# Block differences of weights on GpSimd in place of VectorE, and four seven-product units in place of three in two projection pairs

## The chip, the cores and the metric

The kernel runs on one core of one Trainium2 chip. A core has five engines with a queue of instructions each, which run in order and wait for one another by semaphores: TensorE (PE in the profile; its weight loads are PEld), VectorE (DVE), ScalarE (ACT), GpSimd (POOL) and SyncE (SP, which here only starts transfers). Transfers between the chip's memory (HBM, where the kernel's DRAM tiles lie) and the core's working memory (SBUF) run on 16 DMA engines; they are started from SP's queue and from POOL's. Matrix products are accumulated in banks of a second memory (PSUM).

The metric is the device time of one execution in microseconds (us). The kernel before took 1457.91 us, the median of three runs (1455.56 to 1463.55).

## What is computed

One layer of a decoder trunk on 256 tokens of width 2048, all in float32: a mixer with two attention branches and gates, and a gated feed-forward part with a convolution of width 3.

```python
D_MODEL = 2048; SEQ = 256; D_FF = 5632

def hybrid_mixer(h, w_in, mla_q_norm, mla_w_q_up, mla_kv_norm, mla_w_kv_up,
                 swa_sinks, rel_table, w_o_mla, w_o_swa, w_out):
    c_q, c_kv, k_r, q_s, k_s, v_s, gates = jnp.split(h @ w_in, offsets, axis=-1)
    ...
    o_a = mla_attention(q[..., :MLA_NOPE_DIM], q_rope, kv[..., :MLA_NOPE_DIM], k_rope, kv[..., MLA_NOPE_DIM:])
    o_b = swa_attention(q_s, k_s, v_s, swa_sinks, rel_table)
    g = jax.nn.sigmoid(gates).reshape(B, S, N_BRANCHES, D_MODEL)
    merged = g[:, :, 0] * (o_a @ w_o_mla) + g[:, :, 1] * (o_b @ w_o_swa)
    return merged @ w_out

def conv_ffn(h, w_up, conv_w, conv_b, w_down):
    a, b = jnp.split(h @ w_up, 2, axis=-1)
    ap = jnp.pad(a, ((0, 0), (CONV_WIDTH - 1, 0), (0, 0)))
    c = conv_b
    for j in range(CONV_WIDTH):
        c = c + conv_w[j] * ap[:, j:j + S]
    return (jax.nn.gelu(c, approximate=True) * b) @ w_down

y = hybrid_mixer(rms_norm(x, norm_mix_pre), ...)
x = x + rms_norm(y, norm_mix_post)
y = conv_ffn(rms_norm(x, norm_ffn_pre), ...)
x = x + rms_norm(y, norm_ffn_post)
```

## The kernel before

**Tiling.** The 256 tokens are two tiles of 128. A projection runs over the rows of its weight matrix in blocks of 128 (`k`), and a matrix multiplication takes 128 rows by 128 tokens by 512 columns. Each float32 operand is split into a rounded high part and the remainder, so that one product is three matrix multiplications (`mm3`, lines 199 to 201): high times high, high times low, low times high.

**Chunks and their conversion.** Weights come in chunks of 128 x 1024 (512 KB). SP's queue starts the transfer into a raw tile (lines 143 and 172), ACT writes the high part (`whi`, line 164), and DVE subtracts it from the raw tile for the low part (`wlo`, line 165; both of its inputs lie in SBUF). Then PE multiplies. There are four pairs of `whi` and `wlo` in a ring (`RING = 4`) and three raw tiles (`RAW = 3`), with a few more tiles for one or the other in some stages. A chunk's conversion can start only when PE is done with the chunk four places ahead.

**Pairs and units.** In a "pair" (`pair_gemm`) 1024 columns are made at once. A unit is two row blocks (an even and an odd row chunk). A plain unit (`p` in an order such as `"ppspspsp"`) makes eight products: two row blocks, two token tiles, two column halves. A seven-product unit (`s`) makes seven: it takes sums of the token blocks (made by `token_sums` on DVE and ACT, ahead of time) and differences of the four weight blocks, and adds the partial results at the end (`end_sums`). The differences need four subtractions of 128 x 512. The order string says which units come first; the `s` units always take the first row blocks.

**Where the differences come from.** In two pairs they are made on the spot by `weight_sums` (lines 231 to 234): the gate pair (columns of `w_in`; tiles `gr` for the rows, `gta` and `gtb` for the differences, `cg` and `qg` for the PSUM banks) and the first pair of `w_out` (tiles `mr`, `yg`, `cw`, `qw`). There, POOL's queue starts the transfers of the rows (lines 326 and 327), and the differences are converted as a chunk would be. In the others they are parked: `park_sums` loads two row chunks into a staging tile (line 246, POOL's queue), four subtractions are made in place (line 253), and two stores (lines 258 and 263, POOL's queue) put the differences into DRAM tiles, from where `seven_parked` reads them as chunks later, in all 3.5 chunks for one `s` unit against 2 for a `p` unit. One park is called a quad of subtractions below. Parked are: the latent output pair `a_pair` (matrix `w_o_mla`, tiles `tw`, PSUM banks `ca` and `qa`), and the pairs of `ffn_w_down` (tiles `ta`, `tb` and `tc`, banks `cd`, `cdb`, `cdc`). All parks but the first four use one staging tile (tag `sg`), so that the next park's load waits until the one before has been stored.

**What sets the order.** The code is written against a counter of steps (`now`, `at`, `tick`); a step is one chunk of a projection. `park_sums` puts its subtractions at given steps (`t0` and `t0 + 1`), and the line `tc.keep_in_program_order` pins them to their place in the queue of the engine that makes them. Other instructions are put in order by the scheduler of the framework. At run time each queue goes on as soon as its semaphores let it.

**Stages**, by time in the profiled execution: sliding-window projections and attention to about 198 us; the first output block of that branch, 198 to 240; the gate pair, 240 to 282; the rest of that branch, to 350; latent attention with the other gates, to 550; the latent output pair, 551 to 593; the rest of that matrix with the merge, to 639; the first `w_out` pair, to 682; the rest and the norms, to 770; the first half of the feed-forward projection (steps c = 1 to 5), to 998; two pairs of `ffn_w_down`, to 1120; the second half, to 1340; the last two pairs, to the end.

Of the kernel before, what the change touches and what calls it, by code (L numbers as in the profile page):

```python
# [16 lines left out]
ALU = mybir.AluOpType  # L17
AX = mybir.AxisListType

P = 128  # L20
D = 2048
S = 256
NT = 2
# [19 lines left out]
def trunk_layer(ctx, tc, x, x_cols_in, conv_cols_in, g_mix_post, g_ffn_post, w_in, w_q, w_kv,  # L43
                sinks, rel, wo_a, wo_b, w_out, w_up, w_down, rope_tab, strip_sel, out):
    nc = tc.nc
    vec, act, pe, pool = nc.vector, nc.scalar, nc.tensor, nc.gpsimd
# [10 lines left out]
    base = ctx.enter_context(tc.tile_pool(name="base", bufs=1))  # L57
# [18 lines left out]
    def warm_up(n):  # L76
        for i in range(n):
# [6 lines left out]
                       base=0, channel_multiplier=1)  # L84
# [143 lines left out]

    def weight_sums(even, odd, ta, tb):
        a, b = slice(0, 512), slice(512, 1024)  # L230
        vec.tensor_tensor(ta[:, a], even[:, b], even[:, a], op=ALU.subtract)
        vec.tensor_tensor(ta[:, b], odd[:, b], even[:, b], op=ALU.subtract)
        vec.tensor_tensor(tb[:, a], odd[:, b], ta[:, a], op=ALU.subtract)
        vec.tensor_tensor(tb[:, b], odd[:, a], tb[:, a], op=ALU.subtract)

    staged = set()

    def park_sums(name, w, k, c0, pl, tag, t0, bufs=None):

        td = [dram.tile([P, 1024], F32, name=f"{name}{i}") for i in range(2)]  # L240
        st = []

        def load():
            st.append(sb(pl, [P, D], f"{name}s", tag=tag, bufs=bufs))
            for i in range(2):
                ins = pool.dma_start(st[0][:, i * 1024:(i + 1) * 1024], w[(k + i) * P:(k + i + 1) * P, c0:c0 + 1024])
                if tag not in staged:
                    tc.keep_in_program_order(ins)
            staged.add(tag)

        def less(o, x, y):
            o, x, y = (st[0][:, i * 512:(i + 1) * 512] for i in (o, x, y))
            tc.keep_in_program_order(vec.tensor_tensor(o, x, y, op=ALU.subtract))

        def even():
            less(0, 1, 0)
            less(1, 3, 1)
            pool.dma_start(td[0], st[0][:, 0:1024])

        def odd():  # L260
            less(3, 3, 0)
            less(2, 2, 3)
            pool.dma_start(td[1], st[0][:, 1024:2048])

        at(t0 - 5, load)
        at(t0, even)
        at(t0 + 1, odd)
        return td
# [444 lines left out]
    for g in range(4):  # L713
        acc = gemm(XH, XL, w_in, 0, KT, C_QS + 512 * g, 512)[0] if g else acc_q0
        swa_q(g, acc)
        b = now[0]
# [120 lines left out]
    tb = {0: gate_b(0)}  # L837
# [157 lines left out]
    b = now[0] + 2  # L995
# [8 lines left out]
    for j in range(4):  # L1004
        acc, _ = gemm(XH, XL, w_in, 0, KT, C_GA + 512 * j, 512)
        if j == 3:
            both = sb(base, [P, D], "ta3", tag="sg")
# [100 lines left out]
    yg_all = [[sb(p6, [P, 1024], f"yg_{t}_{j}", tag="f" + "ab"[t], bufs=2) for j in range(2)] for t in range(NT)]  # L1108
    yg = [[yg_all[t][j // 2][:, (j % 2) * 512:(j % 2 + 1) * 512] for j in range(4)] for t in range(NT)]
    ms = {}  # L1110
# [65 lines left out]
    w_done = [0]  # L1176

    def w_place():
# [5 lines left out]
        at(now[0] + 2, *(lambda k=k: late_loads(k) for k in range(4)))  # L1184
        return both[:, 0:1024], both[:, 1024:2048]

    def w_pair():
        d = [yg[t][j] for t in range(NT) for j in range(2)]
        c = pair_gemm("w", w_out, 0, 0, W_ORDER, lambda k, t: (MH_(k)[:, t * P:(t + 1) * P], ML_(k)[:, t * P:(t + 1) * P]),
                      lambda u: ms[u], 0, d, w_place, lambda: [yg_all[t][1] for t in range(NT)])  # L1190

        def pair_evac(i):
            t, j = divmod(i, 2)
            vec.tensor_tensor(d[i], d[i], c[i], op=ALU.add)
            act.activation(jk(f"yj{j}_{t}"), d[i], AF.Square, accum_out=ssy[t][:, j:j + 1])
            vec.tensor_tensor(d[i], d[i], gpost[0][:, j * 512:(j + 1) * 512], op=ALU.mult)

        for i in range(4):
            at(now[0] + i, lambda i=i: pair_evac(i))
# [334 lines left out]
    for i in range(4):  # L1534
        t, j = divmod(i, 2)
# [28 lines left out]


RING = 4
A_ORDER = "ppspspsp"
NA_ = A_ORDER.count("s")
GATE_ORDER = "psppspsp"
B_ORDER = "psspsspssp"  # L1570
B2_ORDER = "ppsspssppp"
NB2 = B2_ORDER.count("s")
# [79 lines left out]
```

## Time and profile before

| | |
|---|---|
| median of three runs | 1457.91 us |
| the profiled execution's own time | 1455.35 us |
| its span, first to last instruction | 1453.6 us |
| PE busy | 1443.9 us, 7522 matrix multiplications |
| DVE busy | 1162.5 us |
| ACT busy | 866.5 us |
| POOL busy | 113.6 us |
| subtractions for block differences, parked | 100 on DVE |
| the same, on the spot | 24 on DVE |

The page of the profile gives each engine's busy time, the share of each 40th of the span, the chain of work that ended last (followed back from the last instruction to what released it), and the costliest groups of instructions as `line engine operation out<-in`, with the count, the busy time, the mean duration in ns, and the idle time ahead of them with what ended it. A view by windows gives the busy time of each engine in a stretch of the span. The timeline gives instructions by start and duration, in brackets the idle time ahead and its releaser.

### The profile page before, as it was taken

The numbers are of one execution on the slowest core, as the hardware profiler recorded it, in microseconds if no ns is written. First come the engines' busy times: TensorE is split into PE (matmuls) and PEld (weight loads), VectorE is DVE, ScalarE is ACT, GpSimd is POOL, SyncE is SP. The second block draws the span as 40 slices with busy tenths as digits, with TensorE's granted clock in tenths as the row PEclk, the third lists the DMA queues.
The fourth block names the chain that finished last, engine by engine and source line by source line (L and its number), as shares of the span: only waits on it lengthen the run. The fifth ranks groups of instructions, "written<-read, shape, count | busy, mean of one in ns | idle before, by whom it ended". The sixth has DMA issues, their size and how long they took to land.

```text
span 1453.6 us, 21420 instructions
## 1 busy us (share of the span) xinstructions
PE 1443.9 (99%) x7522; PEld 1233.6 (85%) x7522; DVE 1162.5 (80%) x2034; ACT 866.5 (60%) x1422; POOL 113.6 (8%) x204
## 2 busy tenths in 40 slices
PE   9999999999999999999999999999999999999997
PEld 7888888888898888888888888888888888888886
DVE  7788896766878775888799899876777797986798
ACT  7588864544555655546576565655646565565673
POOL 0012110010000001100000011000000101010000
PEclk9999999999999999999999999999999999999999
DMA  8755376698775759975666898866878888788965
GB/s 301 218 171 163 104 262 193 218 325 292 245 218 175 231 155 321 353 232 177 216 207 212 266 335 302 279 208 213 310 271 268 307 276 291 248 282 275 356 216 208
DMA packets 164744, 359.74 MB, mean 247 GB/s; under 512 B 20843, under 2 KB 32012, under 8 KB 164636
## 3 DMA queue, kind: packets, MB, share of 16 engines
q1 hardware_dynamic: 143296, 282.76, 59.8%
q0 software_dynamic: 21248, 75.56, 15.1%
q8 instruction: 59, 0.97, 0.3%
q14 instruction: 49, 0.40, 0.1%
q10 hardware_dynamic: 92, 0.05, 0.0%
HBM read 323.67 MB, written 34.65 MB: 247 GB/s over the span
## 4 chain that ended last, share of the span: by engine, by line
PE 97%; DVE 1%; ACT 1%; issue 0%; DVEq 0%; ACTq 0%
PE ub L1345 10%; PE ua L1345 10%; PE accg L199 10%; PE accg L201 10%; PE accg L200 10%; PE ub L1349 5%; PE ua L1349 5%; PE cd L200 2%; PE cd L201 2%; PE cd L199 2%; PE cdc L200 1%; PE cdc L199 1%; PE cdc L201 1%; PE mpo L981 1%; PE cdb L200 1%; PE cdb L199 1%
## 5 line engine op out<-in xcount | busy, mean ns | idle before, releaser
L164 ACT CAST whi<-raw 128x1024 fp32r<-128x1024 f32 (+2 forms) x498 | 504.5, 1022 | 374.7 <-PE accg L201 107.6
L165 DVE TENSOR_TENSOR wlo<-raw,whi 128x1024 fp32r<-128x1024 f32 (+2 forms) x498 | 586.1, 1189 | 176.0 <-ACT whi L164 171.4
L199 PE MATMUL accg<-whi,ahl 128*128 128x512 f32 (+1 forms) x416 | 162.8, 391 | 0.0
L201 PE MATMUL accg<-whi,ahl 128*128 128x512 f32 (+1 forms) x416 | 160.7, 386 | 0.0
L200 PE MATMUL accg<-wlo,ahl 128*128 128x512 f32 (+1 forms) x416 | 159.9, 384 | 0.0
L1345 PE MATMUL ub<-ahl,whi 128*128 128x512 f32 x640 | 154.7, 391 | 0.0
L1345 PE MATMUL ua<-ahl,whi 128*128 128x512 f32 x640 | 154.6, 391 | 0.0
L1345 PEld LDWEIGHTS ub<-ahl,whi 128*128 128x128 f32 x640 | 117.5, 188 | 22.8 <-ACT cc L1237 0.2
L1345 PEld LDWEIGHTS ua<-ahl,whi 128*128 128x128 f32 x640 | 117.5, 188 | 22.7
L199 PE MATMUL accg<-whi,bhl 128*128 128x512 f32 x256 | 100.7, 393 | 0.0
L201 PE MATMUL accg<-whi,bhl 128*128 128x512 f32 x256 | 99.9, 390 | 0.0
L200 PE MATMUL accg<-wlo,bhl 128*128 128x512 f32 x256 | 99.8, 390 | 0.0
L201 PEld LDWEIGHTS accg<-whi,ahl 128*128 128x128 f32 x416 | 78.1, 188 | 15.5
L200 PEld LDWEIGHTS accg<-wlo,ahl 128*128 128x128 f32 x416 | 78.2, 188 | 13.2
L199 PEld LDWEIGHTS accg<-whi,ahl 128*128 128x128 f32 x416 | 78.2, 188 | 12.9
L1349 PEld LDWEIGHTS ub<-ahl,wlo 128*128 128x128 f32 x640 | 82.3, 191 | 3.2
L1349 PEld LDWEIGHTS ua<-ahl,wlo 128*128 128x128 f32 x640 | 82.2, 191 | 3.1
L1349 PE MATMUL ua<-ahl,wlo 128*128 128x256 f32 x640 | 83.7, 283 | 0.0
L1349 PE MATMUL ub<-ahl,wlo 128*128 128x256 f32 x640 | 83.3, 283 | 0.0
L201 PEld LDWEIGHTS accg<-whi,bhl 128*128 128x128 f32 x256 | 48.0, 188 | 10.1
L200 PEld LDWEIGHTS accg<-wlo,bhl 128*128 128x128 f32 x256 | 48.1, 188 | 9.7
L199 PEld LDWEIGHTS accg<-whi,bhl 128*128 128x128 f32 x256 | 48.1, 188 | 9.6
(660 smaller groups left out, 2682.7 us busy)
## 6 DMA issues: line engine op xcount, KB each, us to landing
raw<-in_ffn_w_up_dram SPq DMA_DIRECT2D x142, 512.0 KB, 4.8
raw<-in_w_in_dram SPq DMA_DIRECT2D x105, 512.0 KB, 4.6
raw<-in_ffn_w_down_dram SPq DMA_DIRECT2D x66, 512.0 KB, 5.7
xraw<-in_ffn_w_up_dram SPq DMA_DIRECT2D x34, 512.0 KB, 5.1
raw<-in_w_o_swa_dram SPq DMA_DIRECT2D x32, 512.0 KB, 4.8
raw<-in_w_o_mla_dram SPq DMA_DIRECT2D x26, 512.0 KB, 5.9
raw<-in_w_out_dram SPq DMA_DIRECT2D x26, 512.0 KB, 4.6
ta_s<-in_ffn_w_down_dram POOLq DMA_DIRECT2D x24, 512.0 KB, 6.2
```

Source lines behind the costliest of these rows:

```text
L164: act.copy(hi[:, a:b], raw[:, a:b])
L165: vec.tensor_tensor(lo[:, a:b], raw[:, a:b], hi[:, a:b].bitcast(F32), op=ALU.subtract)
L199: pe.matmul(o, ah, bh, start=start, stop=False)
L200: pe.matmul(o, ah, bl, start=False, stop=False)
L201: pe.matmul(o, al, bh, start=False, stop=stop)
L981: pe.matmul(o, w(t), p_[:, c], start=n == 0, stop=n == 5)
L1345: pe.matmul(acc[i], hi[:, c], hn[p][:, j * 512:(j + 1) * 512], start=p + j == 0, stop=stop)
L1349: pe.matmul(acc[i][:, 0:256], lo[:, c], hn[p][:, j * 512:j * 512 + 256], start=False, stop=False)
```

## The change

All subtractions of `weight_sums` and of `park_sums` are issued to GpSimd. The latent output pair's order goes from three `s` units and five `p` units to four and four, the gate pair's too; each gets one more set of token sums, and the latent output pair one more park. Since `w_out`'s pair would write all its differences to the same two tiles, its second `s` unit gets another tile (`wt`, in the staging tile's place).

```diff
     def weight_sums(even, odd, ta, tb):
         a, b = slice(0, 512), slice(512, 1024)
-        vec.tensor_tensor(ta[:, a], even[:, b], even[:, a], op=ALU.subtract)
-        vec.tensor_tensor(ta[:, b], odd[:, b], even[:, b], op=ALU.subtract)
-        vec.tensor_tensor(tb[:, a], odd[:, b], ta[:, a], op=ALU.subtract)
-        vec.tensor_tensor(tb[:, b], odd[:, a], tb[:, a], op=ALU.subtract)
+        pool.tensor_tensor(ta[:, a], even[:, b], even[:, a], op=ALU.subtract)
+        pool.tensor_tensor(ta[:, b], odd[:, b], even[:, b], op=ALU.subtract)
+        pool.tensor_tensor(tb[:, a], odd[:, b], ta[:, a], op=ALU.subtract)
+        pool.tensor_tensor(tb[:, b], odd[:, a], tb[:, a], op=ALU.subtract)
...
         def less(o, x, y):
             o, x, y = (st[0][:, i * 512:(i + 1) * 512] for i in (o, x, y))
-            tc.keep_in_program_order(vec.tensor_tensor(o, x, y, op=ALU.subtract))
+            tc.keep_in_program_order(pool.tensor_tensor(o, x, y, op=ALU.subtract))
...
+    def w_sums():
+        if w_done[0] % 2:
+            return [yg_all[t][1] for t in range(NT)]
+        both = sb(base, [P, D], "wt", tag="sg")
+        return both[:, 0:1024], both[:, 1024:2048]
+
     def w_pair():
         d = [yg[t][j] for t in range(NT) for j in range(2)]
         c = pair_gemm("w", w_out, 0, 0, W_ORDER, lambda k, t: (MH_(k)[:, t * P:(t + 1) * P], ML_(k)[:, t * P:(t + 1) * P]),
-                      lambda u: ms[u], 0, d, w_place, lambda: [yg_all[t][1] for t in range(NT)])
+                      lambda u: ms[u], 0, d, w_place, w_sums)
...
-A_ORDER = "ppspspsp"
+A_ORDER = "pspspssp"
 NA_ = A_ORDER.count("s")
-GATE_ORDER = "psppspsp"
+GATE_ORDER = "spspspsp"
```

Three places show how instructions move. The first is POOL's queue from the end of the `w_out` pair on (`gpost` are gains that are loaded there, `x_d` is the parked residual stream, `ta_0` and `ta_1` the two DRAM tiles of a park). Before:

```order
L1031 DMA gpost<-in_norm_mix_post_dram 128x512 x4
L1313 DMA x_d<-x_0_5938 128x512 x4
L1313 DMA x_d<-x_1_5939 128x512 x4
L258 DMA ta_0_7945<-ta_s 128x1024
L263 DMA ta_1_7946<-ta_s 128x1024
L246 DMA ta_s<-in_ffn_w_down_dram 128x1024 x2
```

With the change:

```order
L1031 DMA gpost<-in_norm_mix_post_dram 128x512 x4
L246 DMA ta_s<-in_ffn_w_down_dram 128x1024 x2
L253 TENSOR_TENSOR ta_s<-ta_s 128x512 x2
L258 DMA ta_0_7994<-ta_s 128x1024
L253 TENSOR_TENSOR ta_s<-ta_s 128x512 x2
L263 DMA ta_1_7995<-ta_s 128x1024
L246 DMA ta_s<-in_ffn_w_down_dram 128x1024 x2
```

The subtractions stand in POOL's own queue, between a park's load and its stores; nothing of another engine's step stands between one park and the next, and two parks now come ahead of the stores of the residual stream.

The second is DVE's queue in the gate pair (`wlo` from `gr` are the rows' own conversions, from `gta` and `gtb` those of the differences). Before:

```order
L165 TENSOR_TENSOR wlo_2959<-gr_2935,whi_2958 128x512
L165 TENSOR_TENSOR wlo_2966<-gta_2938,whi_2965 128x1024
L231 TENSOR_TENSOR gta_3142<-gr_3139 128x512
L165 TENSOR_TENSOR wlo_2976<-gtb_2939,whi_2975 128x1024
L232 TENSOR_TENSOR gta_3142<-gr_3139 128x512
L165 TENSOR_TENSOR wlo_2988<-raw_2985,whi_2987 128x1024
L165 TENSOR_TENSOR wlo_3006<-raw_3003,whi_3005 128x1024
L165 TENSOR_TENSOR wlo_3024<-raw_3021,whi_3023 128x1024
L165 TENSOR_TENSOR wlo_3042<-raw_3039,whi_3041 128x1024
L233 TENSOR_TENSOR gtb_3143<-gr_3139,gta_3142 128x512
L234 TENSOR_TENSOR gtb_3143<-gr_3139,gtb_3143 128x512
```

With the change:

```order
L165 TENSOR_TENSOR wlo_2923<-gr_2899,whi_2922 128x512
L165 TENSOR_TENSOR wlo_2930<-gta_2902,whi_2929 128x1024
L807 SCALAR_TENSOR_TENSOR tb_0_2707<-tb_0_2707,accg_0_2711 128x512
L807 SCALAR_TENSOR_TENSOR tb_1_2709<-tb_1_2709,accg_1_2712 128x512
L165 TENSOR_TENSOR wlo_2940<-gtb_2903,whi_2939 128x1024
L165 TENSOR_TENSOR wlo_2962<-raw_2959,whi_2961 128x1024
L165 TENSOR_TENSOR wlo_2980<-raw_2977,whi_2979 128x1024
L165 TENSOR_TENSOR wlo_3001<-gr_2995,whi_3000 128x1024
L165 TENSOR_TENSOR wlo_3015<-gr_2995,whi_3014 128x512
L165 TENSOR_TENSOR wlo_3022<-gta_2998,whi_3021 128x1024
L165 TENSOR_TENSOR wlo_3032<-gtb_2999,whi_3031 128x1024
```

The four subtractions between the conversions are gone from DVE, and the second `s` unit follows the first after two plain chunks instead of four.

The third is SP's queue in the latent output pair, at its last `s` units (`araw` is a raw tile of this stage). Before:

```order
L172 DMA raw_6192<-in_w_o_mla_dram 128x1024
L172 DMA raw_6210<-in_w_o_mla_dram 128x1024
L172 DMA raw_6228<-in_w_o_mla_dram 128x1024
L172 DMA araw<-in_w_o_mla_dram 128x512
L172 DMA raw_6248<-tw_0_3736 128x1024
L172 DMA raw_6260<-tw_1_3737 128x1024
L172 DMA araw<-in_w_o_mla_dram 128x1024
```

With the change:

```order
L172 DMA raw_6231<-in_w_o_mla_dram 128x1024
L172 DMA raw_6243<-in_w_o_mla_dram 128x512
L172 DMA raw_6252<-tw_0_3756 128x1024
L172 DMA araw<-tw_1_3757 128x1024
L172 DMA raw_6275<-in_w_o_mla_dram 128x1024
L172 DMA raw_6287<-in_w_o_mla_dram 128x512
L1034 DMA x_0_5969<-in_x_dram 128x512
L172 DMA araw<-tw_0_3758 128x1024
L172 DMA raw_6307<-tw_1_3759 128x1024
```

Two `s` units now stand next to each other: eight loads, seven chunks' worth, for two units, with no plain unit between them (the load of `x` among them is of the residual stream).

## The prediction

> **What bounds the kernel now.** I read the page's first part and its chain of waits first, then the chain's pieces in a steady stretch, then the groups of the two engines that feed PE.
>
> ```profile
> span 1453.6 us, 21420 instructions
> PE 1443.9 (99%) x7522; PEld 1233.6 (85%) x7522; DVE 1162.5 (80%) x2034; ACT 866.5 (60%) x1422; POOL 113.6 (8%) x204
> PE 97%; DVE 1%; ACT 1%; issue 0%; DVEq 0%; ACTq 0%
> L164 ACT CAST whi<-raw 128x1024 fp32r<-128x1024 f32 (+2 forms) x498 | 504.5, 1022 | 374.7 <-PE accg L201 107.6
> L165 DVE TENSOR_TENSOR wlo<-raw,whi 128x1024 fp32r<-128x1024 f32 (+2 forms) x498 | 586.1, 1189 | 176.0 <-ACT whi L164 171.4
> ```
>
> ```profile
> 879.56 3.65 PE ua L1345 x16
> ```
>
> PE is idle for 9.7 us of 1453.6, and 97% of the chain is PE. ACT's conversions wait for PE (374.7 us) and DVE's for ACT: the converters are ahead and held back by the ring. 16 full-width multiplications take 3.65 us, 0.228 each, which is PE's pace. So time leaves this kernel only with multiplications, and enters it wherever the converters fall so far back that PE runs dry. Taking work from DVE alone is worth nothing as long as this holds.
>
> How far ahead they are is the question. In a seven-product unit of the gate pair, where the ring's four places cover less PE time than in plain units:
>
> ```profile
> 263.10 1.23 DVE L165 TENSOR_TENSOR wlo<-gtb,whi 128x1024 fp32r<-128x1024 f32 x1 [1.49 <-ACT whi L164]
> 265.54 0.39 PE L200 MATMUL qg<-wlo,xs 128*128 128x512 f32 x1
> ```
>
> The conversion ends at 264.33 and PE reads it at 265.54: 1.2 us to spare, though DVE had idled 1.49 us just before. This is the margin in the tight places.
>
> **The change part by part.** *Removed from PE.* Two plain units become seven-product units: two products of three multiplications less, 6 x 0.228 = 1.4 us. It is on the path, so the time falls by 1.4.
>
> *Removed from DVE.* 124 subtractions, in 31 quads:
>
> ```profile
> L253 DVE TENSOR_TENSOR ta_s<-ta_s x48: 682/686/697, 290.3 to 937.9; 128x512 f32<-128x512 f32 x48
> L253 DVE TENSOR_TENSOR tb_s<-tb_s x24: 684/686/691, 1128.6 to 1243.6; 128x512 f32<-128x512 f32 x24
> L253 DVE TENSOR_TENSOR tc_s<-tc_s x16: 660/686/689, 494.2 to 1309.7; 128x512 f32<-128x512 f32 x16
> L253 DVE TENSOR_TENSOR tw_s<-tw_s x12: 681/685/692, 375.7 to 465.3; 128x512 f32<-128x512 f32 x12
> L231 DVE TENSOR_TENSOR gta<-gr x3: 679/684/693, 205.4 to 247.3; 128x512 f32<-128x512 f32 x3
> ```
>
> At 0.686 us a quad is 2.74 us and all are 85 us of DVE. Worth 0, since DVE waits for ACT and ACT for PE.
>
> *Added to POOL.* 33 quads (26 parks and 7 on the spot), 132 subtractions. The trace has no such operation of this size on POOL; it has one of half the width, and a copy:
>
> ```profile
> L705 POOL TENSOR_TENSOR bhl<-o,bhl x16: 722/740/1518, 78.2 to 197.4; 128x256 fp32r<-128x256 f32 x16
> L557 POOL COPY gmat<-gx 128x38 f32<-128x38 f32 x1 | 0.2, 215 | 0.8 <-DMA gx<-in_x_cols_dram 0.8
> ```
>
> From 0.215 us at 38 columns to 0.740 at 256 is 2.4 ns a column, so 512 columns take 0.74 + 256 x 0.0024 = 1.36 us. The bounds are 0.74 (width costs nothing) and 1.48 (all is width). I take 1.36: a quad is 5.4 us, all are 180 us, and POOL, busy 113.6 us, has room. [...]
>
> Why L705 reaches 1518 decides what this does to DVE:
>
> ```profile
> 95.77 1.52 POOL L705 TENSOR_TENSOR bhl<-o,bhl 128x256 fp32r<-128x256 f32 x1 [1.69 <-ACT bhl L704]
> 95.46 1.22 DVE L165 TENSOR_TENSOR wlo<-raw,whi 128x1024 fp32r<-128x1024 f32 x1
> 102.48 0.74 POOL L705 TENSOR_TENSOR bhl<-o,bhl 128x256 fp32r<-128x256 f32 x1 [5.19 <-ACT bhl L704]
> 102.83 1.47 DVE L165 TENSOR_TENSOR wlo<-raw,whi 128x1024 fp32r<-128x1024 f32 x1
> ```
>
> At 95.77 POOL starts 0.31 us into a conversion and takes 0.78 more than its 0.74, while the conversion keeps its 1.22. At 102.83 a conversion starts while POOL has 0.39 left and takes 0.25 more. So the two hold each other up, and the later one pays. [...] If DVE always comes second, a quad costs it the full 5.4 us (the upper bound); if POOL does, 0. Conversions alone run 586 us of 1453.6, and with the sums and the feed-forward's own operations DVE does two-input work somewhat over half the time, so I take 60%, 3.2 us a quad. Against the 2.74 it saves, DVE comes out even over the whole kernel. What remains is where the quads go.
>
> *Moved.* On DVE a quad stood at its planned step; on POOL a park follows the one before as soon as the staging tile is free. That cycle is two load issues (1.06), landing, four subtractions with some waiting (about 7), and a store's issue and landing:
>
> ```profile
> ta_s<-in_ffn_w_down_dram POOLq DMA_DIRECT2D x24, 512.0 KB, 6.2
> ta<-ta_s POOLq DMA_DIRECT2D x24, 512.0 KB, 5.2
> 737.04 2.53 POOL L1313 DMA_DIRECT2D x_d<-x  x4 [13.47 <-DVE x L1152]
> 790.97 0.54 POOL L258 DMA_DIRECT2D ta<-ta_s  x1 [51.41 <-DVE ta_s L253]
> 945.90 1.06 POOL L246 DMA_DIRECT2D tb_s<-in_ffn_w_down_dram  x2 [6.48 <-DMA ta<-ta_s]
> ```
>
> In sum 1.1 + 6.2 + 7 + 0.5 + 5.2 = 20 us. Before, the first park of this part was stored at 790.97, and the load of 945.90 waited for its subtractions until 1128.6. With the change two of the 17 parks pass before the residual stream's stores, which still wait for DVE until 737; the 15 left follow at 20 us each and end near 737 + 300 = 1037, inside the first down pair, which had none. The stages:
>
> ```profile
> 198.00:224.00 26.00, 26.00 (x119) 21.47 (x118) 26.00 (x59) 14.82 (x23) 2.40 (x5) 1.00 0.79 272
> 240.00:262.00 22.00, 22.00 (x98) 18.10 (x97) 14.71 (x17) 9.55 (x10) 3.22 (x6) 1.00 0.62 216
> 262.00:290.00 28.00, 28.00 (x124) 23.01 (x124) 21.49 (x23) 18.00 (x20) 1.06 (x2) 1.00 0.58 196
> 550.00:594.00 44.00, 44.00 (x196) 36.44 (x195) 28.38 (x30) 24.39 (x27) 4.45 (x9) 1.00 0.94 338
> 594.00:632.00 38.00, 38.00 (x181) 31.39 (x180) 34.67 (x52) 17.99 (x23) 5.87 (x11) 1.00 0.94 326
> 632.00:683.00 51.00, 51.00 (x231) 42.19 (x230) 41.38 (x49) 26.45 (x29) 2.67 (x5) 1.00 0.56 190
> 790.00:940.00 150.00, 150.00 (x863) 132.40 (x862) 133.28 (x233) 89.35 (x146) 16.01 (x30) 1.00 0.86 291
> 940.00:1000.00 60.00, 60.00 (x344) 52.88 (x343) 43.57 (x76) 33.68 (x57) 1.06 (x2) 1.00 0.71 235
> 1000.00:1040.00 40.00, 40.00 (x178) 32.95 (x177) 27.95 (x32) 22.65 (x29) 0.00 (x0) 1.00 0.69 233
> ```
>
> (After the stretch and its length: busy time and instructions of PE, PEld, DVE, ACT and POOL, granted clock, DMA share, GB/s.)
>
> - *Ahead of the gate pair* (198 to 224) DVE has no idle time. Two quads leave it and two come on POOL: +1 us by the 3.2, and the fourth token sums +2.5 more. It stays hidden by the plain chunks to 240; without that cover, 2 us.
> - *Gate pair* (240 to 290): the third and fourth quads and one park, where one quad stood. Each can use up the 1.2 us margin: 3 x (3.2 - 1.2 - what DVE's idle time, a quarter of the stretch, gives back). I take 1 us (0 to 4). The rows are loaded two units ahead, into two `gr` tiles, so the quads' own length is hidden; with one tile it would not be, 5.4 us a unit.
> - *Latent output pair* (551 to 593): a seven-product unit reads 1.5 chunks more, 0.79 MB, or 2.3 us at 338 GB/s, where DMA is at 0.94 and ACT already waits for it:
>
> ```profile
> ACT whi L164 <- DMA raw<-in_w_o_mla_dram: 10.2, 6, 3.7
> 601.90 1.06 POOL L246 DMA_DIRECT2D ta_s<-in_ffn_w_down_dram  x2 [4.73 <-DVE la L1069]
> ```
>
>   The 1 MB loaded at 601.90 now goes past 660, which helps only behind it. I take 1 us (0 to 3).
> - *Merge and `w_out`* (594 to 690): three quads leave, three come, the first moved up to 602, where DVE is 91% busy, and a park comes to about 671, at the pair's tight end. I take 1 us (0 to 4).
> - *Feed-forward, first half* (740 to 1000): 8 quads become about 13, so per 20 us DVE gives 3.2 in place of 2.9 to 940 (8 x 2.74 in 150 us), and 3.2 in place of 0 after, where DVE idles 16.4 of 60. 0 (0 to 2): the ring is the plain, deep one.
> - *First down pair* (998 to 1040): two parks, 6.4 us of DVE into 12 idle, 4.2 MB more of transfers, on 233 GB/s. I take 1 us (0 to 4). The second half of the feed-forward loses all its quads, for nothing.
>
> The sum is -1.4 + 1 + 1 + 1 + 0 + 1 = +2.6 us: 1455.35 + 2.6 = 1458.0 for an execution like the profiled one. That execution was 2.6 below the median shown, so the median goes from 1457.91 to 1460.5.
>
> **The rivals.** *All is absorbed.* DVE's waits stay inside the margin and only PE's work changes: 1457.91 - 1.4 = 1456.5. For it: not one wait of PE for DVE makes the chain's first 97%. Against: 1.2 us is less than one held conversion.
>
> *The lock makes DVE the bound* (slower). DVE comes second each time, since POOL's four subtractions follow each other: 5.4 us a quad. In the tight places, the three quads of the gate pair, two of merge and `w_out`, two of the first down pair, each then costs PE 5.4 less the margin of 1.2 and about 2 us of idle time: 7 x 2.2 = 15, less 1.4: 1471.5. It decides once a quad's hold on DVE passes what idle time and margin give, about 3.2. For it: DVE is 100% busy from 198 to 224 and 91% from 594 to 632. Against: the conversion at 95.46 shows POOL paying. [...]
>
> *Transfers run ahead into a full stage.* The latent output pair takes its 2.3 us in full and the parks at the first down pair delay its chunks by as much as they move beyond the 338 seen: 233 + 105 is at the limit, some 5 us. 1457.91 - 1.4 + 2.3 + 5 + 2 for the quads = 1465.8.
>
> *DVE's relief shows in PE.* Its 9.7 us of idle time, mostly at both ends, would have to go: 1450 at the very best.
>
> **How the numbers follow.** My sum 0.45, all absorbed 0.17, the lock 0.25, transfers 0.10, relief 0.03. About 0.5%, 7.3 us, is what I count as telling from no change. The first two lie within it (0.62); the lock and the transfers are above it (0.35). The likeliest case's own range is 1456.5 to 1465. The range given, 1455 to 1474, reaches to the lock's price and a little beyond it; what is left out are a larger hold at the top and the relief below.
>
> **What would show it.** Right: 7516 multiplications; lines 231 to 234 and 253 on POOL at 1.3 to 2 us each; line 165's mean above 1189; the last store of a park near 1037 in place of 1310; new idle time of PE, one or two us in all, in the gate pair, around 602, at 671 and past 1000. Wrong: no idle time of PE there (all absorbed); PE waiting for `wlo` many us, with line 165 above 1.4 us in those windows (the lock); PE behind ACT behind DMA at 575 to 600 or 1000 to 1040 (transfers); subtractions at 2 us and more even where DVE idles, which would make my price wrong.

## The result, and the profile after

The changed kernel takes 1495.15 us, the median of six runs (1490.31 to 1496.45), where the kernel before took 1457.62 on the same occasions (six runs, 1455.56 to 1463.55). The ratio is 1.0251, with a 95% interval of 1.0229 to 1.0273: it is slower by some 37 us, well above the range that was given. The profiled execution spans 1491.4 us.

The page of the changed kernel: its span, the engines' busy time, the engines' shares of the chain of waits, and two of the costliest groups (busy time and mean of one, then the idle time before them).

```profile
span 1491.4 us, 21411 instructions
PE 1457.1 (98%) x7516; PEld 1239.2 (83%) x7516; DVE 1192.5 (80%) x1926; ACT 866.7 (58%) x1428; POOL 339.4 (23%) x342
PE 80%; DVE 10%; DMA 4%; issue 3%; ACT 3%; DVEq 0%; ACTq 0%; SPq 0%
L165 DVE TENSOR_TENSOR wlo<-raw,whi 128x1024 fp32r<-128x1024 f32 (+2 forms) x498 | 626.3, 1271 | 192.2 <-ACT whi L164 186.3
L253 POOL TENSOR_TENSOR ta_s<-ta_s 128x512 f32<-128x512 f32 x48 | 81.8, 1705 | 45.5 <-DMA ta_s<-in_ffn_w_down_dram 43.8
```

PE does six multiplications less, and yet is busy 13 us longer. Its idle time rises from 9.7 us to 34.3 (1491.4 less 1457.1). DVE has 108 instructions fewer than before and is busy 30 us longer. A conversion (L165) takes 1.271 us on the mean in place of 1.189, and DVE, which held 1% of the chain, now holds 10%.

Where is it lost? Stretches of the stages that matter, before (first fence) and after (second); behind each loss the changed kernel does the same work later than the kernel before. Columns as in the prediction: stretch and length, busy time of PE, PEld, DVE, ACT and POOL, granted clock, DMA share, GB/s.

```profile
690.00:725.00 35.00, 34.95 (x158) 28.56 (x157) 24.81 (x37) 20.01 (x30) 2.18 (x4) 1.00 0.66 207
755.00:775.00 20.00, 20.00 (x90) 16.57 (x89) 20.00 (x27) 13.06 (x17) 0.00 (x0) 1.00 0.68 210
770.00:790.00 20.00, 20.00 (x119) 17.64 (x118) 16.78 (x27) 12.96 (x20) 0.00 (x0) 1.00 0.60 182
810.00:830.00 20.00, 20.00 (x120) 17.81 (x119) 18.39 (x35) 12.05 (x20) 2.14 (x4) 1.00 0.90 292
870.00:890.00 20.00, 20.00 (x118) 17.71 (x117) 19.61 (x38) 12.16 (x19) 2.13 (x4) 1.00 0.84 282
```

```profile
198.00:224.00 26.00, 22.69 (x95) 17.91 (x95) 25.86 (x45) 10.02 (x17) 13.98 (x13) 0.93 0.64 211
690.00:725.00 35.00, 33.72 (x148) 27.22 (x147) 29.53 (x28) 17.45 (x23) 16.80 (x13) 1.00 0.81 277
770.00:790.00 20.00, 20.00 (x90) 16.58 (x89) 18.47 (x19) 9.61 (x13) 9.25 (x8) 1.00 0.74 254
790.00:810.00 20.00, 19.55 (x107) 16.57 (x106) 19.84 (x21) 10.80 (x14) 12.05 (x8) 1.00 0.74 256
810.00:830.00 20.00, 13.78 (x70) 11.80 (x69) 17.96 (x29) 10.49 (x19) 7.86 (x8) 0.83 0.80 270
905.00:925.00 20.00, 20.00 (x115) 17.60 (x114) 19.66 (x31) 9.74 (x15) 8.69 (x10) 1.00 0.91 308
```

The two largest losses come where DVE's own work had left it no idle time before. In 198 to 224 us it was busy 26.00 of 26 (quoted in the prediction). What it does in about 777 to 808 of the changed kernel, the last steps of a normalisation (`hx`, L1268 and L1270) between conversions, it did in 755 to 775 before, busy 20.00 of 20 (above). PE runs dry behind that: in 810 to 830 it issues 70 multiplications where it issued 120. A full DVE alone isn't enough, though: the work of 870 to 890, where DVE was busy 19.61 of 20, is done in about 905 to 925 with GpSimd working beside it (8.69 us), and PE loses nothing.

What happens inside, on DVE's queue and on POOL's (start, duration, instruction):

```profile
799.91 2.08 DVE L165 TENSOR_TENSOR wlo<-raw,whi 128x1024 fp32r<-128x1024 f32 x1 [0.16 <-ACT whi L164]
801.91 1.79 DVE L418 TENSOR_TENSOR ahl<-hx,ahl 128x512 fp32r<-128x512 f32 x1
803.63 2.26 DVE L1270 TENSOR_TENSOR hx<-hx,row 128x512 f32<-128x512 f32 x1
805.81 2.32 DVE L165 TENSOR_TENSOR wlo<-raw,whi 128x1024 fp32r<-128x1024 f32 x1
808.05 0.68 DVE L418 TENSOR_TENSOR ahl<-hx,ahl 128x512 fp32r<-128x512 f32 x1
```

```profile
796.16 6.99 POOL L253 TENSOR_TENSOR ta_s<-ta_s 128x512 f32<-128x512 f32 x2 [4.45 <-DMA ta_s<-in_ffn_w_down_dram]
804.04 3.01 POOL L253 TENSOR_TENSOR ta_s<-ta_s 128x512 f32<-128x512 f32 x2
```

One quad holds four DVE instructions. Unheld they take 1.22 + 0.68 + 0.68 + 1.22 = 3.80 us; here they take 8.45, so 4.65 us are lost to the hold, in a place where DVE has nothing to spare. As soon as the quad is over, L418 takes its 0.68 again.

DVE is late after that, and two things follow. First the chain of waits behind it (start, duration, what), then PE:

```profile
808.73 2.27 DVE wlo L165 x2
811.00 0.03 DVE cc L1244
811.03 7.71 DMA raw<-in_ffn_w_up_dram
818.74 0.02 issue
818.77 0.02 ACTq L164
818.78 0.04 issue
818.82 1.05 ACT whi L164
```

```profile
809.62 1.11 PE L1355 MATMUL ua<-ahl,wlo 128*128 128x256 f32 x8
816.01 1.09 PE L1289 MATMUL fT<-ident,f 128*128 128x128 f32 x4 [5.28 <-DVE uu L1250]
816.75 2.06 PE L1355 MATMUL ua<-ahl,wlo 128*128 128x256 f32 x8
```

The late conversion gives its raw tile back late, so the next chunk's load lands late (7.71 us on the chain). And PE stands for 5.28 us before a transpose that waits for `uu`, the activation that DVE computes (L1244 to L1250). PE's multiplications keep the program's order here, so a converted chunk behind the transpose cannot help: eight of a chunk's sixteen L1355 run at 809.62, and the other eight start only at 816.75. The stall of 198 to 224 has the same form; its wait is

```profile
PE ckT L747 <- DVE ck L741: 2.6, 1, 2.6
```

(in total, times, longest): a transpose of the compressed key that DVE normalises. Here it isn't the conversions that are held, but six instructions of 128 x 2 elements with which DVE works out that key's norm. Four of them:

```profile
203.19 1.25 DVE L402 TENSOR_TENSOR ck_t<-ck_t,ck_ss 128x2 f32<-128x2 f32 x1
205.95 1.25 DVE L407 TENSOR_TENSOR ck_y<-ck_y,ck_t 128x2 f32<-128x2 f32 x1
207.33 2.94 DVE L401 TENSOR_TENSOR ck_t<-ck_y 128x2 f32<-128x2 f32 x1
212.31 1.25 DVE L410 TENSOR_TENSOR ck_u<-ck_u,ck_t 128x2 f32<-128x2 f32 x1
```

In the kernel before, with no subtraction on GpSimd, each takes 0.15 or 0.16 us. The six take 9.2 us in place of 0.9: a hold cost these short instructions about as much as a conversion.

Third, these stalls are paid again in clock. Windows of the changed kernel just behind three stalls:

```profile
216.00:220.00 4.00, 3.17 (x9) 2.49 (x10) 3.97 (x8) 0.86 (x2) 0.63 (x1) 0.57 0.19 23
740.00:745.00 5.00, 5.00 (x16) 4.21 (x15) 5.00 (x13) 4.06 (x10) 1.90 (x4) 0.50 0.95 296
815.00:820.00 5.00, 3.99 (x16) 3.73 (x17) 4.32 (x8) 3.31 (x6) 1.91 (x2) 0.50 0.90 337
```

In 740 to 745 PE is busy throughout, and starts a full-width multiplication every 0.43 us (742.09, 742.52, 742.94) in place of 0.228. Ahead of the last multiplication the trace has five such stretches at half clock, 23.9 us in all, in which PE is busy for 20.7; half of that, some 10 us, is most of the 13 us of additional busy time.

### The profile page after: what moved, and what is told of

The parts are those of the page before. It is cut to its first block, busy times and chain, and to the rows that moved or that the text cites. A ratio compares the mean times of both kernels' runs of the same rounds, so it can differ in the third digit from the quotient of the medians.

```text
span 1491.4 us, 21411 instructions
## 1 busy us (share of the span) xinstructions
PE 1457.1 (98%) x7516; PEld 1239.2 (83%) x7516; DVE 1192.5 (80%) x1926; ACT 866.7 (58%) x1428; POOL 339.4 (23%) x342
## 4 chain that ended last, share of the span: by engine, by line
PE 80%; DVE 10%; DMA 4%; issue 3%; ACT 3%; DVEq 0%; ACTq 0%; SPq 0%
PE ub L1351 9%; PE accg L199 8%; PE accg L200 8%; PE accg L201 8%; PE ua L1351 8%; PE ub L1355 5%; PE ua L1355 4%; DVE wlo L165 4%; DMA raw<-in_ffn_w_up_dram 2%; PE cd L200 2%; PE cd L201 2%; PE cd L199 2%; ACT whi L164 1%; PE mpo L981 1%; PE cdb L201 1%
## 5 line engine op out<-in xcount | busy, mean ns | idle before, releaser
L165 DVE TENSOR_TENSOR wlo<-raw,whi 128x1024 fp32r<-128x1024 f32 (+2 forms) x498 | 626.3, 1271 | 192.2 <-ACT whi L164 186.3
L253 POOL TENSOR_TENSOR ta_s<-ta_s 128x512 f32<-128x512 f32 x48 | 81.8, 1705 | 45.5 <-DMA ta_s<-in_ffn_w_down_dram 43.8
L1355 PEld LDWEIGHTS ub<-ahl,wlo 128*128 128x128 f32 x640 | 82.2, 191 | 5.2 <-DVE wlo L165 2.0
L1355 PEld LDWEIGHTS ua<-ahl,wlo 128*128 128x128 f32 x640 | 83.0, 193 | 3.1
L1355 PE MATMUL ub<-ahl,wlo 128*128 128x256 f32 x640 | 83.4, 283 | 1.8 <-DVE wlo L165 1.8
L1355 PE MATMUL ua<-ahl,wlo 128*128 128x256 f32 x640 | 84.6, 285 | 0.0
L199 PEld LDWEIGHTS accg<-whi,bhl 128*128 128x128 f32 x256 | 48.4, 189 | 13.5 <-DVE uda L361 3.7
```

Of the source, the lines that this page charges most:

```text
L165: vec.tensor_tensor(lo[:, a:b], raw[:, a:b], hi[:, a:b].bitcast(F32), op=ALU.subtract)
L199: pe.matmul(o, ah, bh, start=start, stop=False)
L253: tc.keep_in_program_order(pool.tensor_tensor(o, x, y, op=ALU.subtract))
L1355: pe.matmul(acc[i][:, 0:256], lo[:, c], hn[p][:, j * 512:j * 512 + 256], start=False, stop=False)
```

## The experiments

The diffs are shortened; `half` and `eng` stand for what the kernels write out at each place. All are compared with runs of the kernel before on the same chip, with its median in brackets; ratios have 95% intervals. "The changed kernel" is the one above, 1495.15 us.

| run | GpSimd's share | us (before) | ratio |
|---|---|---|---|
| e1 | none, new orders | 1461.23 (1456.62) | 1.0029 (1.0018 to 1.004) |
| e2 | all, old orders | 1495.1 (1456.62) | 1.0255 (1.0229 to 1.0281) |
| e3 | 7 on-the-spot quads | 1467.9 (1456.62) | 1.0073 (1.0056 to 1.009) |
| e4 | 26 parks | 1486.16 (1456.62) | 1.0207 (1.0188 to 1.0226) |
| e5 | parks 8 columns wide | 1478.15 (1456.37) | 1.0157 (1.0129 to 1.0185) |
| e6 | parks as memsets | 1479.55 (1456.37) | 1.0151 (1.0132 to 1.017) |
| e7 | parks paced by DVE | 1483.88 (1456.37) | 1.0185 (1.0169 to 1.0201) |
| e8 | parks in quarters | 1484.45 (1456.37) | 1.0189 (1.0172 to 1.0207) |
| e9 | parks narrow, transfers small | 1470.65 (1457.12) | 1.0089 (1.0074 to 1.0105) |
| e10 | 21 quads, not in 680 to 870 | 1472.67 (1457.12) | 1.0106 (1.0085 to 1.0128) |
| e11 | none, gate order alone | 1456.7 (1457.12) | 0.9995 (0.9985 to 1.0005) |
| e12 | parks full, transfers small | 1487.77 (1456.83) | 1.0219 (1.0202 to 1.0236) |

Most of these kernels issue the same 7516 multiplications as e1. So the time at which the same multiplication starts can be subtracted, kernel by kernel; the growth of that difference over a stage is what the stage lost against e1 (us; worked out from the start times in the traces of the profiled executions, stages by e1's time):

| stage (us) | e3 | e5 | e9 | e12 | after | e7 | e8 | e10 |
|---|---|---|---|---|---|---|---|---|
| 150 to 290 | 7.5 | 7.2 | 7.5 | 9.6 | 8.3 | 7.5 | 7.1 | 0.0 |
| 290 to 560 | 0.1 | 0.1 | 0.2 | 1.2 | 1.3 | 0.2 | 0.0 | 1.7 |
| 560 to 640 | 2.0 | 1.8 | 2.1 | 2.3 | 2.4 | 2.3 | 2.2 | 2.4 |
| 640 to 690 | 0.1 | 0.3 | 0.5 | 2.1 | 2.1 | 0.3 | 0.6 | 0.5 |
| 690 to 770 | 0.0 | 2.5 | 0.3 | 0.3 | 5.6 | 0.3 | 4.8 | 0.3 |
| 770 to 850 | 0.0 | 7.7 | 1.6 | 13.5 | 15.9 | 5.5 | 11.6 | 0.3 |
| 850 to 1000 | 0.0 | 0.0 | 0.0 | 0.0 | 0.2 | 0.0 | 0.0 | 0.0 |
| 1000 to 1130 | 0.0 | 0.0 | 0.0 | 0.0 | 0.0 | 0.0 | 0.5 | 15.4 |
| 1130 to the end | 0.3 | 0.0 | 1.0 | 0.8 | 0.1 | 10.4 | 0.0 | 0.0 |

### Orders or GpSimd: e1 and e2

```diff
 e1: the changed kernel, but
-        pool.tensor_tensor(ta[:, a], even[:, b], even[:, a], op=ALU.subtract)
+        vec.tensor_tensor(ta[:, a], even[:, b], even[:, a], op=ALU.subtract)
 ...
-            tc.keep_in_program_order(pool.tensor_tensor(o, x, y, op=ALU.subtract))
+            tc.keep_in_program_order(vec.tensor_tensor(o, x, y, op=ALU.subtract))
 e2: the kernel before, with these lines the other way round
```

> The changed kernel with all 132 subtractions back on VectorE; only the two order strings and the tile for the fourth unit's differences are new. Theory A (GpSimd's subtractions hold up VectorE's conversions, and that is the whole loss): the orders alone are worth their 1.4 us of multiplications, so 1454 to 1458 us, PE idle 8 to 11 us. Rival B (the seven-product units that stand earlier and closer together are what the ring cannot feed): most of the 37 us stays, 1480 us or more.

> The kernel before with all its subtractions on GpSimd and its own orders. Theory A: nearly the whole loss, 1488 to 1500 us. Rival B: near the time before, 1456 to 1465 us.

e2 has the whole loss, 38.5 us: the cause is GpSimd. Alone, the orders cost 4.6 us (e1), where they were expected to gain 1.4; on top of GpSimd's loss they add nothing that shows (1495.15 with them, 1495.1 without). In e1's trace PE is short of 2.45 us at the end of the latent output pair, with the DMA engines at 0.92. It waits for the pair's last sum (`uda`), which stands in DVE's queue behind a conversion, and ACT had waited 4.58 us for that conversion's chunk:

```profile
575.00:600.00 25.00, 22.55 (x100) 18.35 (x99) 18.24 (x21) 13.30 (x14) 2.02 (x4) 1.00 0.92 325
PE accg L199 <- DVE uda L361: 2.5, 1, 2.5
592.18 2.94 ACT L164 CAST whi<-raw 128x1024 fp32r<-128x1024 f32 x3 [4.58 <-DMA raw<-in_w_o_mla_dram]
```

The eight kernels of the table have the same stall, 2.6 to 3.4 us long, and lose another 1.8 to 2.4 us in the row 560 to 640, whichever of them it is, e3 and e9 included. In e3 the stall is 2.8 us; in the changed kernel it is 3.30, and PE's clock is at half behind it (0.71 in 604 to 608); in e1's profiled execution (1457.69, the quickest of its ten) it stays at 1.00 (600 to 640). So the orders cost PE some 2.5 to 5 us at this place. e2 doesn't have this stall, but loses 9.6 us of its own between 560 and 690 against the kernel before (start times again), so the two costs need not add there.

### On the spot or parked: e3 and e4

```diff
 e3: the changed kernel, but
-            tc.keep_in_program_order(pool.tensor_tensor(o, x, y, op=ALU.subtract))
+            tc.keep_in_program_order(vec.tensor_tensor(o, x, y, op=ALU.subtract))
 e4: the changed kernel, but the four lines of weight_sums with vec
```

> The changed kernel with only the seven on-the-spot quads on GpSimd (gate pair and first pair of w_out); the parks are on VectorE at their planned steps. Theory A: the stalls of 198 to 300 us and of 600 to 690 us stay, those of 690 to 900 us go: 1466 to 1476 us. Rival C (the parks, freed from VectorE, run ahead and their transfers are what delays the chunks): near 1457 us, since no park runs ahead.

> The changed kernel with only the parks' 104 subtractions on GpSimd; the seven on-the-spot quads are on VectorE. Theory A: the stalls of 690 to 900 us stay and most of those before go: 1476 to 1486 us. Rival C: nearly the whole loss stays, 1488 us or more.

Against e1 the on-the-spot quads cost 6.7 us and the parks 24.9. e3 lies where theory A had it, but for another reason in part: its loss is the 7.5 us of 150 to 290 (and the 2.0 that go with the orders), and 640 to 690 loses nothing. That the hold, and not the subtractions' later end, makes these 7.5 us is read from the held instructions above; no run separates the two there. e4, at 1486.16, lies between the two theories' figures and decides nothing.

### Hold or transfers: e5, e6, e9, e12

```diff
 e5: the changed kernel, but
-            tc.keep_in_program_order(pool.tensor_tensor(o, x, y, op=ALU.subtract))
+            tc.keep_in_program_order(pool.tensor_tensor(o[:, 0:8], x[:, 0:8], y[:, 0:8], op=ALU.subtract))
 e6: instead
+            tc.keep_in_program_order(pool.memset(st[0][:, o * 512:(o + 1) * 512], 0.0))
 e9: e5, and loads, stores and reads of the parks
+        half = lambda ap: ap.rearrange("p (a n) -> p a n", a=2)[:, :, 0:64]
+        pool.dma_start(half(st[0][:, i * 1024:(i + 1) * 1024]), half(w[(k + i) * P:(k + i + 1) * P, c0:c0 + 1024]))
+        pool.dma_start(half(td[0]), half(st[0][:, 0:1024]))
 ...
-            w_ = convert(raw_row(parked[u][0]), 1024)
+            w_ = convert(raw_row(row(2 * u)), 1024)
 e12: e9, but subtractions of full width, and ahead of the loads
+            pool.memset(st[0], 0.0)
```

> The changed kernel with every queue as it is, but each of the parks' 104 subtractions on GpSimd is 8 columns wide in place of 512: the differences that the parks store are left out but for those 8 columns, so the output isn't the reference's; loads, stores and the run-ahead stay, and GpSimd holds nothing for long. The seven on-the-spot quads keep their full width. Theory A (the hold that a GpSimd subtraction puts on VectorE's two-input instructions is the parks' loss): about the time with only the on-the-spot quads on GpSimd, 1464 to 1472 us, the last store still far ahead of 1310 us. Rival C (the parks' transfers, running ahead, delay the chunks): 1485 us or more, since they now run ahead still further.

> The changed kernel with each of the parks' subtractions replaced by a GpSimd memset of the same 128x512 tile part: the differences are left out, zeros are stored. GpSimd writes the SBUF, but reads nothing there. [...] Rival D (whatever GpSimd runs in SBUF holds VectorE): line 165 stretched by the rest of the memset, and a loss in proportion to the memset's length against the subtraction's 1.3 us.

> The changed kernel with the order of TensorE's, VectorE's and ScalarE's queues untouched, but with parks that neither hold nor move much: subtractions 8 columns wide, loads and stores an eighth of their size, and the parked chunks read from rows of the same matrix in place of the parked differences, so those differences are left out of the output. The on-the-spot quads stay. Rival C for the 10 us that stayed with narrow subtractions (the parks' transfers, run ahead at 297 to 318 GB/s into 700 to 725 and 770 to 800 us, make the raw chunks late): these 10 us go, 1464 to 1470 us. Rival B2 (VectorE's queue is in another order where no subtractions stand between its instructions, and that is what stalls): they stay, 1475 to 1481 us.

> As the kernel with light parks (loads and stores an eighth of their size, parked chunks read from rows of the same matrix, so the differences are left out), but with the parks' subtractions at their full width on GpSimd again; a GpSimd memset fills the staging tile ahead of each load. So the hold without the transfers, the fourth corner beside narrow subtractions with full transfers (1478), neither (1470.6) and both (1495). If hold and transfers add up: 1470.6 + 17 = 1488, 1484 to 1492 us. If they need each other (a held conversion is absorbed as long as the raw chunks come early): 1472 to 1480 us.

e5 missed theory A's range: without any long hold 10 us stayed over e3. They lie in two stages. The windows of e5, and then of e9:

```profile
690.00:725.00 35.00, 34.23 (x151) 27.96 (x150) 23.80 (x28) 18.00 (x26) 4.52 (x10) 1.00 0.86 303
770.00:790.00 20.00, 20.00 (x94) 16.69 (x93) 17.75 (x24) 10.78 (x14) 6.10 (x9) 1.00 0.92 318
790.00:810.00 20.00, 15.56 (x89) 13.91 (x88) 13.38 (x22) 11.27 (x18) 4.44 (x11) 0.86 0.88 297
```

```profile
690.00:725.00 35.00, 35.00 (x156) 29.00 (x155) 27.51 (x30) 19.75 (x28) 3.47 (x7) 1.00 0.72 237
770.00:790.00 20.00, 20.00 (x97) 16.89 (x96) 19.93 (x27) 13.12 (x16) 8.20 (x10) 1.00 0.73 215
790.00:810.00 20.00, 20.00 (x121) 17.72 (x120) 15.80 (x30) 11.22 (x20) 7.39 (x15) 1.00 0.68 197
```

In e5 the DMA engines are at 0.92 with 318 GB/s in 770 to 790, where the kernel before had 0.60 with 182, and DVE in the next window has 6.6 us of idle time: it is not held, it has nothing to convert. ACT in the same trace waits for the raw chunk:

```profile
783.56 1.05 ACT L164 CAST whi<-raw 128x1024 fp32r<-128x1024 f32 x1 [3.61 <-DMA raw<-in_ffn_w_up_dram]
```

e9, with the same queues of PE, DVE and ACT, but small transfers, has PE busy throughout these windows again and 1470.65 us in all, 0.65 above rival C's range: the transfers make 7.5 of these 10 us, and rival B2 is out. So both theories were right in part. e12 closes the square of four:

| parks | transfers small | transfers full |
|---|---|---|
| narrow (no hold) | 1470.65 | 1478.15 |
| full width (hold) | 1487.77 | 1495.15 |

The hold costs 17.1 us on the left and 17.0 on the right; the transfers cost 7.5 above and 7.4 below. They add up, as the first of e12's two forecasts had it. (e12's memsets, 1.81 us each, stand in GpSimd's queue besides, but hold nothing: the 18 conversions that started beside one take 1.216 us at the median.)

e6 stays above theory A's 1464 to 1472 us as e5 does, and for the same reason, since its transfers are full: it loses 2.3 and 7.6 us in 690 to 770 and 770 to 850, where e5 loses 2.5 and 7.7. What it tells is in the conversions. Of all full-width conversions of each trace, those that started while a park's or an on-the-spot operation of GpSimd was running (counts and medians from the traces):

| kernel | GpSimd's shortest operation, us | conversions started beside one | their median, us | alone, us |
|---|---|---|---|---|
| after | 1.26 | 57 | 2.115 | 1.224 |
| e8 | 0.45 | 118 | 1.473 | 1.222 |
| e6, beside its memsets alone | 0.52 | 16 | 1.225 | 1.224 |

Beside a memset, which reads nothing, a conversion isn't held at all (the longest of the 16 takes 1.227). Rival D falls.

### The length of one instruction, and the pace: e8 and e7

```diff
 e8: the changed kernel, but
-            tc.keep_in_program_order(pool.tensor_tensor(o, x, y, op=ALU.subtract))
+            for n in range(0, 512, 128):
+                tc.keep_in_program_order(pool.tensor_tensor(o[:, n:n + 128], x[:, n:n + 128], y[:, n:n + 128], op=ALU.subtract))
 e7: the changed kernel, but at the start of each half quad
+            tc.keep_in_program_order(vec.memset(ramp[:, 2 * j:2 * j + 1], 0.0))
+            tc.keep_in_program_order(pool.tensor_copy(ramp[:, 2 * j + 1:2 * j + 2], ramp[:, 2 * j:2 * j + 1]))
```

> The changed kernel with each of the parks' subtractions on GpSimd cut into four of 128 columns (by the 0.215 us at 38 columns and 0.740 at 256 about 0.43 us each, so 1.7 us for 512 in place of 1.3). Theory A1 (VectorE waits for the end of the one GpSimd instruction that runs, and then goes first): a hold is 0.4 us in place of 1.09, and the time falls to 1472 to 1484 us. Theory A2 (GpSimd goes on with its next one while VectorE waits): the hold is the whole quad's, longer than before, 1497 us or more.

> The changed kernel with the parks' subtractions on GpSimd, but each half quad waits for a one-column memset that VectorE does at the step at which the kernel before had the subtractions: no run-ahead. Theory A: a quad at such a place takes 2.74 us from VectorE and holds it for up to 4 x 1.09 = 4.4 us, so at most 1.6 us a quad and 8 quads in 790 to 940 us: 1468 to 1481 us. Rival C (run-ahead is the loss): 1466 to 1470 us. Rival E (any quad in a dense stretch costs its full hold): 1483 us or more.

e8, half a microsecond above A1's range and far from A2's, speaks for A1. A held conversion loses 0.25 us in place of 0.89, though GpSimd spends more time in all, and 6.3 us over the narrow parks remain of the hold's 17. e7's total lies where rival E had it, just above A. Its stages say otherwise: without run-ahead 690 to 770 loses 0.3 in place of 5.6, and 770 to 850 loses 5.5 in place of 15.9. But it pays 10.4 us after 1130, in the last steps of the second half, where quads now come that had been done by 1037. So the total speaks for E and the stages against it (850 to 1130 lose nothing), and what makes that late place tight wasn't followed further.

### Only where there is room, and the order alone: e10 and e11

```diff
 e10: the changed kernel, weight_sums with vec, and
-            tc.keep_in_program_order(pool.tensor_tensor(o, x, y, op=ALU.subtract))
+            eng = vec if tag == "sg" and name in ("ta4_", "ta5_", "ta6_", "ta7_", "ta8_") else pool
+            tc.keep_in_program_order(eng.tensor_tensor(o, x, y, op=ALU.subtract))
 e11: the kernel before, but
-GATE_ORDER = "psppspsp"
+GATE_ORDER = "spspspsp"
```

> The changed kernel with 21 of its 33 quads on GpSimd: the seven on-the-spot quads and the five parks of ffn_w_down that fall into 680 to 870 us are on VectorE at their steps; the later parks wait behind these and run ahead only from about 880 us. Theory F (a hold and a transfer cost something only where VectorE or DMA has no idle time, and 890 to 1040 us has enough): the time of the orders alone, 1458 to 1463 us. Rival E (each quad on GpSimd costs its hold wherever it stands): 21 quads at about 1 us, 1478 us or more.

> The kernel before with the gate pair's order alone, all subtractions on VectorE. The orders' loss of some 4 us sits in the latent output pair by the profile (575 to 600 us, where a seven-product unit reads 1.5 chunks more): then this one is worth its three multiplications, -0.7 us, 0.998 to 1.001 of the time before. If the gate pair's fourth quad on VectorE costs too: 1.002 or more.

In e10 the losses of 150 to 290 and of 690 to 850 are gone with 12 of 33 quads taken off GpSimd (0.0, 0.3 and 0.3 in the table). Rival E falls with that: 21 quads are still there. But theory F misses too: the time is 1472.67, since the later parks, now from 896 us on, run into the first down pair (the profiled execution, 1477.21, was the slowest of four, so the 15.4 of the table is at the upper end):

```profile
1025.00:1050.00 25.00, 20.36 (x81) 14.84 (x82) 18.82 (x15) 10.96 (x14) 9.95 (x10) 1.00 0.87 303
1050.00:1075.00 25.00, 24.41 (x107) 19.61 (x106) 22.75 (x19) 16.14 (x17) 8.49 (x8) 1.00 1.02 385
```

```profile
1006.50 12.12 DMA raw<-ta
1019.65 1.05 ACT whi L164
1024.01 4.04 DVE wlo L165 x3
1028.22 1.00 issue
1029.22 1.23 DVE wlo L165
1030.46 7.81 DMA raw<-ta
1038.37 1.06 ACT whi L164
```

(windows, and the longest pieces of the chain of waits.) A chunk lands after 12.12 us, and PE has 20.36 of 25. PE waits there for `wlo`, behind late chunks and behind DVE at once; which of the two weighs more isn't separated. So the stretch that forgave everything in the changed kernel, whose last quad starts at 1030 us, does not forgive parks that go on to 1128.

e11 is not to be told from the kernel before. None of these kernels beats it.

## Why the prediction was wrong

**PE, -1.4.** The multiplications fell to 7516 as forecast. The seven-product unit that was added to the latent output pair costs more than the two added units bring: its term of +1 (0 to 3) should have been 2.5 to 5. The mechanism, 1.5 chunks more on DMA engines at 0.94, was right as far as e1's chain shows it: a late chunk, a late conversion, a late `uda`. The gate pair's unit costs nothing that could be measured (e11).

**DVE's relief, 0.** Right: e9 takes DVE from 1175.7 us (e1) to 1123.2, with neither the parks' hold nor most of their transfers, and isn't faster than e3 (1470.65 and 1467.9).

**GpSimd's price and the hold, 1.36 and 3.2 us.** Right as means. A subtraction alone takes 1.26 to 1.31. DVE lost 132 subtractions of 0.685, 90 us, and is still 16.8 us busier than in e1: 107 us for 33 quads, 3.25 a quad. But the mean isn't what decided: the two quads of 202 to 217 us cost DVE 8.3 us in the six small instructions alone, and the one of 796 to 807 costs it 4.65. That the one that comes second pays is what the conversions show: those that started beside a subtraction take 2.115 us at the median, and those within which a subtraction began keep their 1.22 at the median. The 60% behind the 3.2 counts work with two inputs alone, and no run shows that restriction: in the changed kernel's trace L406, which reads one tile, takes 1.26 us beside a subtraction in place of 0.16 before, while L958, with one tile too, takes 0.28 three times, as it does alone.

**Feed-forward, first half, 0 (0 to 2).** This is the step that failed: in place of 0 to 2 us, 770 to 850 lost 15.9, and the 5.6 us of 690 to 770, for most of which the sum had no term, are the parks' too (e3, without them, loses nothing there). The balance of 3.2 us taken against 2.9 given was a mean over 790 to 940. But the quads that ran ahead fell on what DVE did before that, in 755 to 775, where it had no idle time, and no row of the prediction covers 683 to 790. Against e1, the first L1268 of that work starts 20.1 us late and the last L1270 26.8 us late. The second half of the step, "the ring is the plain, deep one", covers `wlo` alone. PE waited for `uu`, which DVE makes as well and which no ring of converted chunks covers.

**Ahead of the gate pair, 0 (2 without cover).** It lost some 5.4 of the 8.3 us of 150 to 290; the other 3 lie in the gate pair, inside its own term's range (0 to 4). The 26.00 of 26 was read and quoted, but the two quads were priced by conversions, and the instructions that were held are small ones in front of `ck`. The cover assumed to hide the rest, PE's plain chunks to 240, stands in PE's queue behind a transpose that waits for DVE.

**Transfers.** The end of the parks near 1037 us was right to the microsecond (the last subtraction ends at 1037.6), and partly by luck: the last fifteen quads start at 759.6, not 737, and follow one another every 19.4 us, not 20, the first with its load already done. But their traffic was weighed only in the latent output pair and in the first down pair, and there the changed kernel loses nothing to them. It costs 7.5 us in 690 to 850, where six parks run in place of three, and that had no term. e10 shows that the first down pair was a real danger; the parks were through just in time.

**The clock** had no term either. Of the 35.7 us between the spans of e1 and the changed kernel (1455.7 and 1491.4), 22.0 are idle time of PE and 13.7 are multiplications that took longer (1457.1 less 1443.4, for the same 7516).

**The rivals.** The lock, DVE held by GpSimd's subtractions, was the right mechanism with the wrong places and too low a price: 15 us for seven tight quads, where the hold costs 17.1 for the parks and 6.7 with the quads on the spot. The transfers were right in kind too. Each was priced as if it came alone, and they add up. From one kernel to the next: 4.6 (e1) + 6.7 (e3) + 17.1 (e12 less e9) + 7.5 (e5 less e9) + 2.7 for what the small parks still cost (e9 less e3) = 38.6, against 37.5 between the two medians. That hold and transfers add up is shown by the four kernels around e12; that the orders' 4.6 is a share of its own isn't, since e2 loses 38.5 without them. The range went to the dearer rival, not to the sum. What was said to show the lock, PE waiting for `wlo` many us, wasn't the sign either; it waited some 5 us for `wlo`, and 17.4 for `uu`, `uda`, `x` and `ck`.

## What to carry to other kernels

Look for the short stretches in which an engine has no idle time (here 20 us, not 150) before giving it or its neighbour work that can delay it; a mean over a stage hides them. Look also at the stretches into which work that runs ahead will move, not only at those that it leaves. For each wait of the bound engine ask which of its inputs have a ring in front of them: a lead in converted chunks doesn't cover an in-order queue that next needs something else. Work that is moved to a free engine also loses the pace that the busy one gave it, so its transfers must be placed anew, and losses in different stretches add up.

## What the runs showed of the hardware

- A full-width conversion that started while GpSimd ran a subtraction was in most cases held to that subtraction's end: in the changed kernel's trace 50 of 57 end 1.08 to 1.10 us behind it, the other seven keep 1.21 to 1.23 us in all. The loss at the median is 0.89 us beside subtractions of 1.26, 0.25 beside those of 0.45, and none beside memsets of 0.52. Short instructions paid as much (128 x 2 elements: 1.25 us in place of 0.15). L401 at 207.33, begun while GpSimd issued a transfer, took 2.94 us, to the end of the second subtraction behind it (210.24). One that takes an operand from PSUM paid nothing (L1373, from `ub`: 0.41 us beside a subtraction, 16 times, and 0.42 alone).
- PE's clock fell to half behind some stalls of less than three microseconds and not behind others: after 2.59 us without work near 214 us the granted clock is 0.57 in 216 to 220, after 2.67 near 737 it is 0.50 in 740 to 745, and after 1.76 near 879 it is 0.77 and 0.81 in 880 to 884 and 884 to 888; after 2.58 near 833 it stays 1.00. In the changed kernel's trace the changes of the granted clock ahead of PE's last multiplication lie at whole steps of 3.41 us from one another. In the step before each of its five falls PE had been idle for 1.76 to 3.25 us, and in no step that was followed by one at full clock for more than 1.50. The stall near 833 lies across two steps (1.41 and 1.17 us).
